# The low part of every second weight load: from a VectorE subtraction to an accumulating DMA

## The chip, the cores and the metric

The kernel runs on one core of one Trainium2 chip. Its time is the device time of one execution in microseconds (us); lower is better. The engines are named as in the profile: PE (TensorE: matmuls; PEld are its weight loads), ACT (ScalarE), DVE (VectorE), POOL (GpSimd), SP (SyncE, which here issues the DMAs).

## The reference: what is computed

Two layers of a decoder over 256 tokens of width 2048, in float32. Layer 0 mixes a causal multi-scale pooling with attention to a memory of 256 tokens; layer 1 has differential attention over shared keys and values, and memory attention again. Each layer ends with a squared-ReLU feed-forward of width 8192. Most of the work is products of the 256 tokens with large weight matrices, used once each:

```python
for i in range(DEPTH):                       # 2
    u = rms_norm(x, mix_norm[i]) @ w_in[i]   # 2048 x 2048
    ...
    x = x + jnp.concatenate([token_out, mem_out], axis=-1) @ w_out[i]
    x = x + squared_relu_mlp(rms_norm(x, ffn_norm[i]), w_ff1[i], w_ff2[i])   # 2048 x 8192 x 2048
```

## The kernel before

**The weights are a stream.** The host lays all weight matrices out as 5796 blocks of 128 x 128 in the order of their use, 8 blocks (1024 columns, 512 KB) to one load: 725 loads, called halves here. The class `Feed` (lines 42 to 100) streams them. `load` issues the DMA of a half from SP into one of 4 buffers named raw (line 60). `fill` works by quarters of 4 blocks (512 columns, two to a half): it makes a high part `hi` by a cast to the matmul's input type float32r on ACT (line 76), and a low part `lo`, what the cast lost, by a subtraction on DVE (line 77); each has 4 buffers of one quarter. `fill(q)` runs before quarter q is used and prepares the quarters up to q + 3 (`AHEAD`); each quarter first asks for the loads up to three halves further on (line 72).

**The matmuls.** The activations are split into a high and a low part as well, side by side (512 columns). `a_part` (lines 216 to 224) and the second matrix of the feed-forward (lines 495 and 496) take two matmuls to a block: `hi` with 512 columns, `lo` with 256. Where the tokens are the output rows, `wide_step` (lines 236 to 244) takes six matmuls of 512 columns to a quarter.

**The order of the work.** Each engine works through its own queue in the order of the program, and the program is written as the stream goes: `fill` is called from the matmul loops, and other work is hung between the quarters by `at` and `tick` (lines 121 to 127). An engine's queue stands still while its first instruction waits for a buffer, a load or another engine. A buffer is given to the next tile of its name in turn, once the last reader of the old tile is done.

**The feed-forward** (`ffn`, lines 460 to 513) is the largest part: in each of the two layers 4 passes of `up` (first matrix, 16 chunks of 16 blocks, that is two halves each) and 4 of `down` (second matrix, the same size). A chunk of `up` ends with a copy on ACT (line 473), an addition and a product on DVE (lines 475 and 476, the latter through the helper of line 141), a square and a cast on ACT (lines 478 and 479) and a subtraction on DVE (line 480). A chunk of `down` ends with two additions on DVE (lines 451 and 452). Squares for the row norms are summed on POOL (`add_square`, lines 437 to 448). In layer 1 the memory is loaded again into raw buffers (`mem_again`, lines 681 to 688).

Of the kernel before, what the change touches and what calls it, by code (L numbers as in the profile page):

```python
# [10 lines left out]
F32 = mybir.dt.float32  # L11
F32R = mybir.dt.float32r
BF16 = mybir.dt.bfloat16
AF = mybir.ActivationFunctionType
ALU = mybir.AluOpType
# [3 lines left out]
P = 128  # L19
T = 256  # L20
# [8 lines left out]

# columns of the parameter array  # L30
G_MIX, G_MEM, G_FFN, G_KV = 0, 32, 64, 96
G_PS, G_MQ, G_MK, G_QN, G_KN, G_SUB = 112, 124, 126, 128, 129, 130
G_QR, G_KR = 131, 163
NPAR = 195
# columns of the constant array
C_ID, C_MASK, C_COS, C_SIN, C_INV = 0, 128, 256, 288, 320
# [4 lines left out]

class Feed:
    """Streams the weights in the order of use: load, split into a high and a low part."""

    AHEAD = 3

    def __init__(self, nc, wst, wpool):
        self.nc, self.wst, self.wpool = nc, wst, wpool
        self.order = []
        self.pos = 0  # L50
        self.loaded = 0
        self.raw = {}
        self.split = {}
        self.done = 0

    def load(self, upto):
        while self.loaded < min(upto, NH):
            h = self.loaded
            n = min(1024, (NBLK - 8 * h) * P)
            t = self.wpool.tile([P, 1024], F32, tag="raw", bufs=4, name=f"raw{h}")  # L60
            step = 512 if h == 0 else 1024
            for c in range(0, n, step):
                m = min(step, n - c)
                self.nc.sync.dma_start(t[:, c : c + m], self.wst[h, :, c : c + m])
            self.raw[h] = t
            self.loaded += 1

    def fill(self, q):
        nq = NBLK // 4
        while self.done < min(q + 1 + self.AHEAD, nq):  # L70
            i = self.done
            self.load(i // 2 + 4)
            src = self.raw[i // 2][:, (i % 2) * 512 : (i % 2) * 512 + 512]
            hi = self.wpool.tile([P, 512], F32R, tag="hi", bufs=4, name=f"hi{i}")
            lo = self.wpool.tile([P, 512], F32R, tag="lo", bufs=4, name=f"lo{i}")
            self.nc.scalar.copy(hi, src)  # L76
            self.nc.vector.tensor_sub(lo, src, hi.bitcast(F32))  # L77
            self.split[i] = (hi, lo)
            if i % 2:
                del self.raw[i // 2]  # L80
            self.done += 1
# [22 lines left out]
def trunk(ctx: ExitStack, tc: tile.TileContext, xT, memT, par, lam, cst, wst, yT):  # L104
# [11 lines left out]

# [1 line left out]
    pend = {}  # L118
# [13 lines left out]

# [1 line left out]
    def vt(name, bufs=8):  # L134
        return tp.tile([P, T], F32, tag="v", bufs=bufs, name=name)
# [6 lines left out]

# [1 line left out]
    param = cp.tile([P, NPAR], F32, name="param")  # L144
# [37 lines left out]
    def rsqrt(out, mean):  # L182
        """out = 1/sqrt(mean + EPS), [128, 256], mean in PSUM; one Newton step."""
        l = vt("rs_l")
        nc.scalar.activation(l, mean, AF.Ln, bias=eps)
        h = vt("rs_h")
        nc.scalar.activation(h, l, AF.Exp, bias=lnc, scale=-0.5)
        t = vt("rs_t")
        nc.scalar.activation(t, h, AF.Square)
        t2 = vt("rs_t2")  # L190
        stt(t2, mean, EPS, t, ALU.add, ALU.mult)
        stt(out, t2, 3.0 * CN * CN, h, ALU.subtract, ALU.mult, reverse0=True)

    def rsqrt_cols(out, v):
        """out = 1/sqrt(v), a few columns of SBUF, v holding EPS already"""
        n = v.shape[-1]
        w = [tp.tile([P, 16], F32, tag="w8", bufs=8, name="rc")[:, :n] for _ in range(4)]
        nc.scalar.activation(w[0], v, AF.Ln)
        nc.scalar.activation(w[1], w[0], AF.Exp, bias=lnc, scale=-0.5)
        nc.vector.tensor_mul(w[2], w[1], w[1])  # L200
        nc.vector.tensor_mul(w[3], w[2], v)
        stt(out, w[3], 3.0 * CN * CN, w[1], ALU.subtract, ALU.mult, reverse0=True)
# [11 lines left out]

# [1 line left out]
    def a_part(ps, w, l, n, ks, xs, first=True, last=True):  # L216
# [9 lines left out]
    def c_tile(ps, w, l, n, ks, xs):  # L226
        """as a_part, with all three products summed in ps[:, :256]"""
        for i, k in enumerate(ks):
            hi, lo = feed.block((w, l, k, n, 1))
            nc.tensor.matmul(ps[:, 0:T], hi, xs[:, k, 0:T], start=i == 0, stop=False)  # L230
            nc.tensor.matmul(ps[:, 0:T], hi, xs[:, k, T : 2 * T], start=False, stop=False)
            nc.tensor.matmul(ps[:, 0:T], lo, xs[:, k, 0:T], start=False, stop=i == len(ks) - 1)
            if feed.pos % 4 == 0:
                tick()
# [14 lines left out]

# [1 line left out]
    def rstd_from(name):  # L251
# [6 lines left out]
    def columns(name):  # L258
        """1/rms of the tokens, token by partition, and its square"""
        st = stat("tc_" + name)  # L260
        for i in range(2):
            nc.tensor.matmul(
                st[:, 2 * i : 2 * i + 2], acc[name][:, i * P : i * P + P], ones_d[:, 0:2],
                start=True, stop=True,
            )
        v = tp.tile([P, 2], F32, tag="m2", bufs=12, name="cv")
        nc.vector.tensor_scalar_add(v, st[:, 0:4].rearrange("p (a b) -> p a b", b=2)[:, :, 0], EPS)
        col = cp.tile([P, 2], F32, tag="c_" + name, name="c_" + name)
        rsqrt_cols(col, v)
        col2 = cp.tile([P, 2], F32, tag="d_" + name, name="d_" + name)  # L270
        nc.vector.tensor_mul(col2, col, col)
        return col, col2

# [1 line left out]
    def key_rows(ps, cols, d):  # L275
        """ps: two token tiles [128, 512] in PSUM; returns them with heads of d normalised"""
        n = 512 // d
# [19 lines left out]
    def query_rows(ps, cols, d):  # L297
        """the two token tiles as they are, and y[token, (t, head)], the scale of their scores"""
        raw = tp.tile([P, 2, 512], F32, tag="rows", bufs=2, name="qrow")
# [53 lines left out]
    def turn_rows(raw, i, dst, g):  # L353
        """chunks i, i+1 of the rows -> dst [128 features, 2, 256 tokens], times g"""
        t4 = pp.tile([P, 2, T], F32, tag="t", bufs=1, name="tr")
        for c in range(2):
            for t in range(2):
                nc.tensor.transpose(
                    t4[:, c, t * P : t * P + P], raw[:, t, (i + c) * P : (i + c) * P + P], ident
                )  # L360
        nc.scalar.activation(dst, t4, AF.Copy, scale=g)

# [1 line left out]
    def mem_query(src, gq, cols):  # L364
        """src PSUM [128 d, 256]: the queries of one head before their norm, which scales
        the scores; returns them times the gain, and that scale"""
        q = tp.tile([P, T], F32, tag="q", bufs=2, name="mq")
# [21 lines left out]
    def mem_head(q, y, k, v, e, pT, out, lag):  # L389
        """q [128 d, 256] and the scale y[token, block] of its scores; k [128 d, 256],  # L390
        v(mb) -> [128 m, 128 d]; out: split chunk"""

# [42 lines left out]

# [1 line left out]
    def add_square(key, src, first, act=False):  # L437
        """adds the square of a chunk to acc[key]"""
        if first:
            acc[key] = tp.tile([P, T], F32, tag="acc", bufs=2, name="acc")  # L440
            nc.gpsimd.tensor_mul(acc[key], src, src)  # L441
            return
        sq = tp.tile([P, T], F32, tag="psq", bufs=2, name="psq")
        if act:
# [13 lines left out]

# [1 line left out]
    def ffn(l, xs, sz):  # L460
# [53 lines left out]

    # =============== layer 0 ===============
    big = sp.tile([P, 6144], F32, tag="big", name="big0")
# [24 lines left out]

    # keys and values of the memory together, one block row after another
    mem_chunk(0)
# [92 lines left out]
    def out_tiles(l, cat, lead, ks, fx, between):  # L636
        """the output projection; three chunks start on the parts in `lead`, ks come last"""
        first = [mmt("wo") for _ in range(3)]
# [34 lines left out]

    # =============== layer 1 ===============
    kv = sp.tile([P, 6144], F32, tag="big", name="big1")
# [5 lines left out]
    def mem_again(p):  # L681
        t = wp.tile([P, 4, T], F32, tag="raw", bufs=4, name="memraw1")
        nc.sync.dma_start(t, memT[:, 4 * p : 4 * p + 4, :])
        for k in range(4):
            at(
                6 + 2 * k,
                lambda k=k: split_gain(mems1[:, 4 * p + k, :], t[:, k, :], gcol(G_MEM + 16 + 4 * p + k)),
            )
# [63 lines left out]

    # -lambda and the gain behind the heads
    lp = lamt.rearrange("p (a d) -> p a d", a=4)
# [206 lines left out]
```

## Time and profile before

| | us |
|---|---|
| time, median of 2 runs (2113.99 to 2115.19) | 2114.59 |
| span of the profiled execution, first to last instruction | 2112.8 |
| PE busy | 2099.1 (99%) |
| PEld busy | 1814.1 (86%) |
| DVE busy | 1485.7 (70%) |
| ACT busy | 1196.4 (57%) |
| POOL busy | 126.5 (6%) |
| DMA engines, mean busy share of the weights' queue | 56.6% |

No time of its own was kept for the profiled execution beside its span; the median of the runs stands 1.8 us above that span. In rows of groups, "out<-in" names the tiles, x the number of instructions, then come busy us, mean ns of one, and the idle time before them with what ended it. In rows of stretches each engine's busy us stands with its number of instructions, then the granted PE clock, the busy share of the DMA engines and GB/s. In a timeline a row has its start, its duration, engine, line and operation.

### The profile page before, as it was taken

The page shows a single profiled execution, that of the slowest core. Times are in us where ns is not written, and L with a number is a line of the kernel's source. Part 1 is how long each engine was busy: PE and PEld are TensorE (multiplying, and loading weights), DVE is VectorE, ACT ScalarE, POOL GpSimd, SP SyncE. Part 2 cuts the span into 40 slices and gives each one's busy share as a digit, 9 for nine tenths or more (in the row PEclk, how much of TensorE's full clock was granted, in tenths as well). Part 3 has the DMA queues.
Part 4 walks back from the last instruction along what each step waited for, and adds up shares of the span by engine and source line. Part 5 has one row for each costly group of instructions (what it writes and reads, how often), then busy time and mean ns, then how long its engine had stood idle before and what let it go on. Part 6 is the DMA issues. An engine that isn't in the chain of part 4 may idle for free.

```text
span 2112.8 us, 33195 instructions
## 1 busy us (share of the span) xinstructions
PE 2099.1 (99%) x11758; PEld 1814.1 (86%) x11758; DVE 1485.7 (70%) x2788; ACT 1196.4 (57%) x2351; POOL 126.5 (6%) x145
## 2 busy tenths in 40 slices
PE   8999999999999999999999999999999999999999
PEld 6788888888888888888888778888888888888888
DVE  8787876766666666687755687876676666666665
ACT  6665566654564564455655577556664565465443
POOL 7001300000000000032000000310000000000000
PEclk9999999999999999999999999999999999999999
DMA  7546555555555555556565432555555555555564
GB/s 246 181 155 188 187 189 190 190 190 189 192 190 190 191 190 191 189 184 197 188 227 191 142 116 95 179 185 190 190 190 191 191 190 190 189 190 190 189 205 160
DMA packets 110471, 390.81 MB, mean 185 GB/s; under 512 B 12256, under 2 KB 14944, under 8 KB 110304
## 3 DMA queue, kind: packets, MB, share of 16 engines
q1 hardware_dynamic: 110304, 388.69, 56.6%
q8 instruction: 92, 1.51, 0.3%
q14 instruction: 75, 0.61, 0.1%
HBM read 386.54 MB, written 2.10 MB: 184 GB/s over the span
## 4 chain that ended last, share of the span: by engine, by line
PE 97%; DVE 1%; DMA 1%; ACT 1%; issue 0%; SPq 0%; DVEq 0%; ACTq 0%
PE ff L219 22%; PE ff L495 22%; PE ff L220 11%; PE ff L496 11%; PE wo L219 6%; PE wo L220 3%; PE u L219 2%; PE u L220 1%; PE k L241 1%; PE q L241 1%; PE k L243 1%; PE v L241 1%; PE k L242 1%; PE v L242 1%; PE v L243 1%; PE q L243 1%
## 5 line engine op out<-in xcount | busy, mean ns | idle before, releaser
L77 DVE TENSOR_TENSOR lo<-raw,hi 128x512 fp32r<-128x512 f32 x1449 | 1018.8, 707 | 495.4 <-ACT hi L76 469.9
L76 ACT CAST hi<-raw 128x512 fp32r<-128x512 f32 x1449 | 898.3, 621 | 808.3 <-PE ff L495 355.7
L219 PE MATMUL ff<-fx,hi 128*128 128x512 f32 x2048 | 710.9, 393 | 0.0
L495 PE MATMUL ff<-z,hi 128*128 128x512 f32 x2032 | 704.7, 392 | 0.0
L220 PE MATMUL ff<-fx,lo 128*128 128x256 f32 x2048 | 570.4, 279 | 0.0
L496 PE MATMUL ff<-z,lo 128*128 128x256 f32 x2032 | 565.9, 279 | 0.0
L219 PEld LDWEIGHTS ff<-fx,hi 128*128 128x128 f32 x2048 | 383.5, 187 | 86.8
L495 PEld LDWEIGHTS ff<-z,hi 128*128 128x128 f32 x2032 | 380.5, 187 | 86.0
L220 PEld LDWEIGHTS ff<-fx,lo 128*128 128x128 f32 x2048 | 385.7, 188 | 0.1
L496 PEld LDWEIGHTS ff<-z,lo 128*128 128x128 f32 x2032 | 382.7, 188 | 0.0
L219 PE MATMUL wo<-cat,hi 128*128 128x512 f32 x512 | 182.3, 400 | 0.0
L220 PE MATMUL wo<-cat,lo 128*128 128x256 f32 x512 | 143.8, 281 | 0.0
L219 PEld LDWEIGHTS wo<-cat,hi 128*128 128x128 f32 x512 | 96.1, 188 | 23.9 <-DVE cat L141 0.3
L220 PEld LDWEIGHTS wo<-cat,lo 128*128 128x128 f32 x512 | 96.8, 189 | 0.1
L480 DVE TENSOR_TENSOR z<-ff_z,z 128x256 fp32r<-128x256 f32 x128 | 54.5, 426 | 40.8 <-ACT z L479 40.7
L219 PE MATMUL u<-xs,hi 128*128 128x512 f32 x192 | 69.7, 405 | 0.0
L441 POOL TENSOR_TENSOR acc<-resid 128x256 f32<-128x256 f32 x4 | 3.6, 894 | 1096.1 <-DVE resid L452 625.5
L451 DVE TENSOR_TENSOR resid<-resid,ff 128x256 f32<-128x256 f32 x127 | 53.5, 421 | 21.9 <-PE ff L496 20.4
L448 POOL TENSOR_TENSOR acc<-acc,psq 128x256 f32<-128x256 f32 x75 | 65.1, 873 | 20.0 <-ACT psq L445 15.2
L478 ACT ACTIVATE ff_z<-ff_y 128x256 f32<-128x256 f32 x128 | 53.5, 418 | 21.7 <-DVE ff_y L141 21.7
L141 DVE SCALAR_TENSOR_TENSOR ff_y<-ff_y,r_x 128x256 f32<-128x256 f32 x128 | 54.6, 426 | 4.3
L452 DVE TENSOR_TENSOR resid<-resid,ff 128x256 f32<-128x256 f32 x127 | 53.5, 421 | 4.3
(243 smaller groups left out, 1954.2 us busy)
## 6 DMA issues: line engine op xcount, KB each, us to landing
raw<-in_w SPq DMA_DIRECT2D x723, 512.0 KB, 3.4
resid<-in_x SPq DMA_DIRECT2D x8, 256.0 KB, 4.5
memraw<-in_mem SPq DMA_DIRECT2D x4, 512.0 KB, 4.7
out_y<-resid SPq DMA_DIRECT2D x16, 128.0 KB, 2.9
memraw<-in_mem SPq DMA_DIRECT2D x7, 256.0 KB, 4.5
raw<-in_w SPq DMA_DIRECT2D x3, 256.0 KB, 3.4
memraw<-in_mem SPq DMA_DIRECT2D x2, 128.0 KB, 3.1
const<-in_cst SPq DMA_DIRECT2D x1, 168.0 KB, 4.0
```

The lines of the kernel that those rows point to most:

```text
L76: self.nc.scalar.copy(hi, src)
L77: self.nc.vector.tensor_sub(lo, src, hi.bitcast(F32))
L141: nc.vector.scalar_tensor_tensor(out=out, in0=a, scalar=s, in1=b, op0=op0, op1=op1, **kw)
L219: nc.tensor.matmul(ps, hi, xs[:, k, :], start=first and i == 0, stop=False)
L220: nc.tensor.matmul(ps[:, T : 2 * T], lo, xs[:, k, 0:T], start=False, stop=last and i == len(ks) - 1)
L241: nc.tensor.matmul(ps[t], xl, hi, start=k == 0, stop=False)
L243: nc.tensor.matmul(ps[t], xh, lo, start=False, stop=k == NK - 1)
L448: nc.gpsimd.tensor_add(acc[key], acc[key], sq)
L451: nc.vector.tensor_add(resid[:, n, :], resid[:, n, :], ps[:, 0:T])
L480: nc.vector.tensor_sub(z[:, i, T : 2 * T], z2, z[:, i, 0:T].bitcast(F32))
L495: nc.tensor.matmul(ps, hi, z[:, i, :], start=a, stop=False)
L496: nc.tensor.matmul(ps[:, T : 2 * T], lo, z[:, i, 0:T], start=False, stop=b)
```

## The change

Odd halves from 9 to 721 (`summed`) get their low part another way. ACT casts the whole half to `his` in one copy of 1024 columns, ACT multiplies `his` by -1 into `los`, and a DMA issued from POOL loads the same half from memory a second time and adds it to `los` on its way. Even halves, and the first 8 and the last, are split as before. The copy, the product and the DMA of a half are issued 6 quarters ahead (`EARLY`) by `begin`. To make room in on-chip memory, several pools of buffers are smaller: raw 3 in place of 4, hi and lo 2 each in place of 4, beside 2 buffers each of his and los of one half; the small tiles of `vt` 5 in place of 8, psq 1 in place of 2. Comments are taken out, which moves line numbers. The diff, cut to what acts:

```diff
     AHEAD = 3
+    EARLY = 6
...
+        self.begun = 0
+        self.high = {}
+
+    def summed(self, h):
+        return h % 2 == 1 and 8 <= h < NH - 2
 
     def load(self, upto):
...
-            t = self.wpool.tile([P, 1024], F32, tag="raw", bufs=4, name=f"raw{h}")
+            t = self.wpool.tile([P, 1024], F32, tag="raw", bufs=3, name=f"raw{h}")
...
+    def begin(self, upto):
+        while self.begun < min(upto, NH):
+            h = self.begun
+            if self.summed(h):
+                self.load(h + 1)
+                hi = self.wpool.tile([P, 1024], F32R, tag="his", bufs=2, name=f"his{h}")
+                self.nc.scalar.copy(hi, self.raw[h])
+                lo = self.wpool.tile([P, 1024], F32R, tag="los", bufs=2, name=f"los{h}")
+                self.nc.scalar.mul(lo, hi.bitcast(F32), -1.0)
+                self.nc.gpsimd.dma_start(lo, self.wst[h], accum_op=ALU.add)
+                self.high[h] = hi, lo
+            self.begun += 1
+
     def fill(self, q):
         nq = NBLK // 4
         while self.done < min(q + 1 + self.AHEAD, nq):
             i = self.done
-            self.load(i // 2 + 4)
-            src = self.raw[i // 2][:, (i % 2) * 512 : (i % 2) * 512 + 512]
-            hi = self.wpool.tile([P, 512], F32R, tag="hi", bufs=4, name=f"hi{i}")
-            lo = self.wpool.tile([P, 512], F32R, tag="lo", bufs=4, name=f"lo{i}")
-            self.nc.scalar.copy(hi, src)
-            self.nc.vector.tensor_sub(lo, src, hi.bitcast(F32))
+            self.load(i // 2 + 3)
+            self.begin((i + self.EARLY) // 2)
+            h, c = i // 2, slice((i % 2) * 512, (i % 2) * 512 + 512)
+            src = self.raw[h][:, c]
+            if self.summed(h):
+                hi, lo = (x[:, c] for x in self.high[h])
+            else:
+                hi = self.wpool.tile([P, 512], F32R, tag="hi", bufs=2, name=f"hi{i}")
+                self.nc.scalar.copy(hi, src)
+                lo = self.wpool.tile([P, 512], F32R, tag="lo", bufs=2, name=f"lo{i}")
+                self.nc.vector.tensor_sub(lo, src, hi.bitcast(F32))
             self.split[i] = (hi, lo)
...
-    def vt(name, bufs=8):
+    def vt(name, bufs=5):
...
-        sq = tp.tile([P, T], F32, tag="psq", bufs=2, name="psq")
+        sq = tp.tile([P, T], F32, tag="psq", bufs=1, name="psq")
...
-        t = wp.tile([P, 4, T], F32, tag="raw", bufs=4, name="memraw1")
+        t = wp.tile([P, 4, T], F32, tag="raw", bufs=3, name="memraw1")
```

More of the change, by code (lines that the diff above doesn't have):

```diff
@@ L71, in fill @@
             i = self.done
-            self.load(i // 2 + 4)
-            src = self.raw[i // 2][:, (i % 2) * 512 : (i % 2) * 512 + 512]
-            hi = self.wpool.tile([P, 512], F32R, tag="hi", bufs=4, name=f"hi{i}")
-            lo = self.wpool.tile([P, 512], F32R, tag="lo", bufs=4, name=f"lo{i}")
-            self.nc.scalar.copy(hi, src)
-            self.nc.vector.tensor_sub(lo, src, hi.bitcast(F32))
+            self.load(i // 2 + 3)
[9 more added lines that the diff above has]
+                self.nc.vector.tensor_sub(lo, src, hi.bitcast(F32))
             self.split[i] = (hi, lo)
             if i % 2:
-                del self.raw[i // 2]
+                del self.raw[h]
+                self.high.pop(h, None)
             self.done += 1
```

## The prediction

> **What bounds the kernel now.** I read the page first (busy times, chain, groups), then the stretch of one feed-forward stage, then the tile of the loaded weights.
>
> ```profile
> span 2112.8 us, 33195 instructions
> ...
> PE 2099.1 (99%) x11758; PEld 1814.1 (86%) x11758; DVE 1485.7 (70%) x2788; ACT 1196.4 (57%) x2351; POOL 126.5 (6%) x145
> ...
> PE 97%; DVE 1%; DMA 1%; ACT 1%; issue 0%; SPq 0%; DVEq 0%; ACTq 0%
> ...
> L77 DVE TENSOR_TENSOR lo<-raw,hi 128x512 fp32r<-128x512 f32 x1449 | 1018.8, 707 | 495.4 <-ACT hi L76 469.9
> L76 ACT CAST hi<-raw 128x512 fp32r<-128x512 f32 x1449 | 898.3, 621 | 808.3 <-PE ff L495 355.7
> ```
>
> TensorE (PE) is busy in 2099.1 of 2112.8 us and carries 97% of the chain. The splitting of the weights on ACT and DVE waits for PE and not the reverse. So the kernel can gain at most the 13.7 us in which PE is idle, 0.6%, unless its matmuls change, and the diff touches none. Relief for DVE (70% busy) is worth nothing here. What counts is whether weights still come in time. The next row, busy times by stretch, gives the pace at which PE eats them.
>
> ```profile
> core 0: us, PE busy (x) PEld busy (x) DVE busy (x) ACT busy (x) POOL busy (x), PEclk, DMA share, GB/s
> 400.00:800.00 400.00, 400.00 (x2310) 352.69 (x2309) 267.75 (x473) 219.60 (x409) 0.00 (x0) 1.00 0.58 190
> ```
>
> Two matmuls go to a block: 1155 blocks in 400 us, 0.346 us each. A load ("half", 8 blocks) lasts 2.77 us on PE, two halves 5.54 us.
>
> **The change, part by part.** From half 9 to half 721 every odd half, 357 of them, becomes "summed" (S); even ones stay "plain" (P). I write P1 S1 P2 S2 for their order of use. S loses two casts and two subtractions and gains a copy and a multiplication by -1 of 1024 columns on ACT, and one DMA issued by POOL that adds the load to the result. By these rows from the groups with shapes kept apart,
>
> ```profile
> L475 DVE TENSOR_TENSOR ff_y<-ff,ff_c 128x256 f32<-128x256 f32 x128 | 53.5, 418 | 0.0
> ...
> L141 DVE SCALAR_TENSOR_TENSOR ff_y<-ff_y,r_x 128x256 f32<-128x256 f32 x128 | 54.6, 426 | 4.3
> ...
> L478 ACT ACTIVATE ff_z<-ff_y 128x256 f32<-128x256 f32 x128 | 53.5, 418 | 21.7 <-DVE ff_y L141 21.7
> ...
> L479 ACT CAST z<-ff_z 128x256 fp32r<-128x256 f32 x128 | 52.0, 406 | 4.1
> L473 ACT COPY ff_c<-ff 128x256 f32<-128x256 f32 x128 | 46.6, 364 | 0.0
> ...
> L283 ACT ACTIVATE ksq<-krow 128x512 f32<-128x512 f32 x10 | 6.3, 631 | 0.0
> ```
>
> a cast grows by (621-406)/256 = 0.84 ns a column, so the copy of 1024 takes 621+512x0.84 = 1051 ns; an activation by 0.83, so the multiplication takes 631+512x0.83 = 1056 ns. ACT goes up by 357x(1.05+1.06-2x0.62) = 310 us to 1507, DVE down by 357x2x0.707 = 505 to 981. No engine but PE fills the span, and busy time decides nothing.
>
> The buffers decide. Raw buffers go from 4 to 3, so the load of S2 takes the place of P1 and must wait for the last reader of P1, the subtraction of its second quarter on DVE. And ACT works in program order: copy of S2, multiplication of S2, cast, cast of P2, copy of S3. The casts of P2 thus stand behind the copy of S2, which waits for the load of S2, which waits for P1. That closes a ring which gives one turn for each pair of halves, without PE in it. Its steps come from these rows: the tile of the raw weights in a quiet stretch, then a timeline.
>
> ```profile
> L77 DVE TENSOR_TENSOR lo<-raw,hi x73: 683/692/693, 599.4 to 699.1; 128x512 fp32r<-128x512 f32 x73
> L76 ACT CAST hi<-raw x73: 615/622/627, 600.0 to 699.9; 128x512 fp32r<-128x512 f32 x73
> ...
> DMA to landing us min/median/max: 3.1/3.3/4.1
> ```
>
> ```profile
> 799.70 0.62 ACT L76 CAST hi<-raw 128x512 fp32r<-128x512 f32 x1 [0.61 <-PE ff L219]
> ...
> 800.36 0.69 DVE L77 TENSOR_TENSOR lo<-raw,hi 128x512 fp32r<-128x512 f32 x1 [0.54 <-ACT hi L76]
> ...
> 801.08 8.65 SPq L64 DMA_DIRECT2D raw<-in_w  x4
> ```
>
> Hops: ACT to DVE 800.36-800.32 = 0.04, DVE to SP 801.08-801.05 = 0.03; for ACT to ACT I take 0.03 and for landing to ACT 0.04, after these. One turn where PE runs the second matrix of the feed-forward: end of P1's subtraction, hop 0.03, load 3.3, hop 0.04, copy 1.05, hop 0.03, multiplication 1.06, two casts 1.24, hop 0.04, subtraction 0.69: **7.48 us against PE's 5.54**. In the first matrix the copy L473 stands between multiplication and casts, and L475, L141 stand on DVE before the two subtractions. The way over DVE is the longer: the last part is 0.36+0.04+0.42+0.03+0.43+0.69+0.69 = 2.66 in place of 1.97, and the turn 8.17. For the other stages, whose ACT and DVE have as much side work, I take 8.17 too.
>
> What the accumulating DMA adds to this ring is its traffic. It starts after the multiplication, 2.0 us before the next S load is issued. No row shows such a DMA. The nearest are two plain loads in close order, in the DMA queue's timeline and the landings of the same two windows, and the highest rate:
>
> ```profile
> 1075.84 0.33 SPq L64 DMA_DIRECT2D raw<-in_w  x1
> ```
>
> ```profile
> raw<-in_w SPq DMA_DIRECT2D x1, 512.0 KB, 3.4
> ```
>
> ```profile
> 1076.63 0.33 SPq L64 DMA_DIRECT2D raw<-in_w  x1
> ```
>
> ```profile
> raw<-in_w SPq DMA_DIRECT2D x1, 512.0 KB, 4.0
> ```
>
> The first landed at 1079.24 as if alone, the second at 1080.63: a load occupies the DMA engines for about 1.3 us (1.39 here, 1.25 at the 419 GB/s of the busiest slice below), and 2.0 us of its 3.3 are latency.
>
> ```profile
> GB/s 0 151 231 348 232 348 392 408 419 399 224 385 339 284 14 44 350 347 373 354 219 367 67 216 221 63 318 143 11 281 57 90 356 333 283 79 384 111 314 224
> ```
>
> An accumulate reads the weights and the old value, so I take twice, 2.6 us. If POOL and the queue need 1 to 2 us before data flows, those 2.6 us meet the 1.3 us of the next S load. Bounds on the delay: 0 if they pass each other; 2.6 if the load must wait for all of it. I take 1.3, an even share of the engines while both run: nearest to the second load above, which waited for the part of its neighbour that was still running. Nothing excludes a slower accumulate; that is a rival.
> One rule speaks against the change. The Trainium skill, "Collectives: The Full Stack", section on the bandwidth ceiling, says that a summing DMA costs no extra arithmetic but reads two sources on the same read ring, so it ran at about half the rate of a copy. By it an accumulate would take twice a plain load; no run here shows it yet. The Trainium skill, "DMA: Bandwidth & Descriptors", section on issuing engines, adds that POOL's DMAs run on the same 16 engines as SP's; by it the collision is real, and the delay of 0 would need luck in timing.
>
> Latency of the accumulate itself (L, from the end of the multiplication) is not in the ring: PE gets S late but evenly. It enters only through the two buffers of the copied S: S3's copy waits until PE is done with S1, two turns for 2.14+L+2.77, so L counts only above 13.5 us at a turn of 9.2.
>
> Smaller parts, together: casts of P wait for PE four quarters back as before (2 buffers over half the quarters). The 8 to 5 and 2 to 1 buffers serve work that has a whole turn of slack; should squares on POOL come late behind the waiting DMA issue, the row statistic at the end of a stage waits one turn, four times, under 40 us. On SP the load of P3 stands behind the waiting load of S2, lands about 4.0+1.3 us after its issue, and is wanted 6 us after it.
>
> **Sum.** At its start the kernel is not yet in pairs:
>
> ```profile
> 0.00:29.00 29.00, 16.69 (x51) 10.20 (x52) 14.01 (x16) 9.52 (x16) 0.94 0.80 279
> ```
>
> 51 matmuls with high parts by 29 us, 4 a quarter: half 8 starts near 33 us; with 10 us at the end the 357 pairs take 2070 us, 5.80 each. The feed-forward has 128 pairs with each matrix (8 passes of 16 chunks of 2 halves), 101 pairs remain. Mean turn with 1.3 us of delay: (128x8.78 + 229x9.47)/357 = 9.22. Increase 357x(9.22-5.80) = 1221 us. On the profiled 2112.8 that is 3334; the median of the runs stands 1.8 above that span, so **3336 us**. Delay 0 gives 2872, delay 2.6 gives 3800. With the fastest landing (3.1) and no side work in the ring it would be 7.28 a turn, 2643.
>
> **Rivals.** (1) The other side: PE stays the bound and the time stays at 2115. The ring would have to close in 5.54 us, so the load would have to land 1.36 us after its issue; the fastest in the quiet stretch took 3.1. Chance 0.04, with 0.01 of it for a gain over 2%, which the 0.6% of idle PE hardly allows.
> (2) The clock. PE would be idle over 3 us a turn, and this happened early in the run:
>
> ```profile
> 21.52 0.64 PE L243 MATMUL mk<-lo,mems 128*128 128x512 f32 x1 [1.87 <-DVE lo L77]
> ...
> 22.00:24.00 2.00, 2.00 (x6) 1.62 (x5) 2.00 (x3) 0.62 (x1) 1.84 (x3) 0.50 0.20 33
> ```
>
> After a gap of 1.87 us the granted clock was 0.50. If it stayed there, a pair would take 2x5.80 = 11.6 us and the kernel 2114.6+357x5.80 = 4185. Half a clock for only 3 us a turn costs PE 1.5 us and hides in its idle time. The Trainium skill, "TensorE: Matmul & The Clock Gate", section on the HAM clock gate, wants an idle window of about 3.4 us first; the trace did it after less. Chance 0.08.
> (3) The accumulate is itself the bound: slow in POOL's issue or in the DMA engines. It decides above L = 13.5 us; at L = 20 a turn is 12.5 us and the time 2114.6+357x6.7 = 4500. No row speaks for it or against it. Chance 0.10.
> (4) That the DMAs are not issued at all is excluded: POOL's queue holds 357 of them.
>
> **How the numbers follow.** The ring with its collision has 0.78, own range 2643 to 3800, likeliest 3336. The range for 8 in 10 runs from 2750 to 4000: it leaves out rival 1 (0.04), the thin low end of the ring (0.04) and most of rivals 2 and 3 (0.12). A difference under 2% can't be told from none in this measurement: slower 0.96, within 2% 0.03, faster 0.01.
>
> **What would show it.** Right: SP's load issue waits for DVE's subtraction once a pair; ACT's longest wait is the copy of S for the raw load; PE busy near 65%, waiting for the S low part; S loads land in about 4.6 us, not 3.3. Wrong: PE still at 99%; ACT waiting for PE rather than the load; PEclk near 5 in most slices; or S loads landing in 3.3 with PE waiting on accumulates that land after 14 us.

## The result and the profile after

The changed kernel takes 2430.01 us (median of 2 runs, 2424.87 to 2435.16) against 2114.59 before: a ratio of 1.1488, 95% interval 1.1429 to 1.1548. Slower was forecast; 3336 us was not. The profiled execution spans 2433.1 us, and its rows are read against that span.

The page of the changed kernel: engines, the load of the DMA engines in 40 slices, the DMA queues, the chain of work that ended last, by engine and by line.

```profile
span 2433.1 us, 32615 instructions
...
PE 2207.2 (91%) x11758; PEld 1847.2 (76%) x11758; DVE 1014.9 (42%) x2074; ACT 1440.5 (59%) x2351; POOL 422.8 (17%) x502
...
DMA  8889999999998999999879965999999998898997
...
q0 software_dynamic: 51408, 187.19, 45.2%
q1 hardware_dynamic: 110304, 388.69, 44.7%
...
DMA 45%; PE 33%; ACT 10%; issue 9%; POOL 2%; DVE 1%; ACTq 0%; POOLq 0%; DVEq 0%
DMA los<-in_w 37%; DMA raw<-in_w 8%; ACT his L82 6%; PE ff L522 6%; PE ff L246 5%; PE ff L523 3%; PE ff L247 3%; ACT los L84 3%; PE wo L246 2%; PE u L246 1%; PE wo L247 1%; PE q L270 1%; PE q L268 1%; PE q L269 1%; PE v L270 1%
```

PE has become an engine that waits a little: it was idle for 13.7 us and is now for 225.9 (2433.1 - 2207.2); its busy time grew by 108 us with the same 11758 matmuls. The chain was 97% PE and is 45% DMA, 37% of it accumulates on their way and 8% plain loads. The two queues are the reason to look at: q1 (all loads, from SP) holds 44.7% of the span of the 16 DMA engines, 1.50 us for each of 725 loads (some 40 smaller transfers of the same queue are counted in); q0 (the accumulates, from POOL) 45.2%, that is 0.452 x 2433.1 / 357 = **3.08 us each**. Together they fill 89.9%, and 0.93 in the stretch of the feed-forward below.

Groups and DMA issues of the changed kernel, then a stretch of the feed-forward (columns as in the prediction).

```profile
L82 ACT CAST his<-raw 128x1024 fp32r<-128x1024 f32 x357 | 375.1, 1051 | 840.9 <-PE ff L522 289.5
...
L85 POOL DMA_DIRECT2D los<-in_w x357 | 309.0, 865 | 1952.6 <-ACT los L84 961.5
...
L84 ACT ACTIVATE los<-his 128x1024 fp32r<-128x1024 f32 x357 | 378.2, 1060 | 9.7
...
raw<-in_w SPq DMA_DIRECT2D x723, 512.0 KB, 5.3
los<-in_w POOLq DMA_DIRECT2D x357, 512.0 KB, 7.2
```

```profile
400.00:800.00 400.00, 364.49 (x1983) 308.68 (x1981) 143.51 (x283) 230.44 (x348) 53.78 (x63) 0.98 0.93 245
```

From issue to landing, a plain load now takes 5.3 us (3.4 before), an accumulate 7.2. In 400 us PE does 1983 matmuls where it did 2310, with the DMA engines at 0.93 where they were at 0.58. What PE waits for is shown by its three longest waits (us in total, times, longest):

```profile
PE ff L523 <- DMA los<-in_w: 86.2, 68, 3.5
PE ff L247 <- DMA los<-in_w: 56.9, 69, 4.8
PE v L270 <- DMA los<-in_w: 23.2, 7, 6.3
```

All rows of this kind together make 214 of PE's 226 idle us: nearly every wait of PE ends with the landing of an accumulate.

The prediction's ring asks which buffer a load waits for. These are timelines of the copy of one summed half, of the load issued behind it with its landing, of the copy of the next summed half, and of the next plain half; the second copy `his` ends at 700.26, the subtraction `lo` at 703.73.

```profile
692.96 1.05 ACT L82 CAST his<-raw 128x1024 fp32r<-128x1024 f32 x1 [1.65 <-DMA raw<-in_w]
```

```profile
694.04 0.33 SPq L72 DMA_DIRECT2D raw<-in_w  x1
```

```profile
raw<-in_w SPq DMA_DIRECT2D x1, 512.0 KB, 5.1
```

```profile
699.21 1.05 ACT L82 CAST his<-raw 128x1024 fp32r<-128x1024 f32 x1 [2.04 <-DMA raw<-in_w]
700.29 0.33 SPq L72 DMA_DIRECT2D raw<-in_w  x1
```

```profile
702.45 1.28 DVE L103 TENSOR_TENSOR lo<-raw,hi 128x512 fp32r<-128x512 f32 x2
...
703.76 0.33 SPq L72 DMA_DIRECT2D raw<-in_w  x1
```

One load goes out 0.03 us after the copy of a summed half, the next 0.03 us after the last subtraction of a plain one, and so on in turn. Which load is which is told by its landing: the one issued at 694.04, when the copy of one summed half had ended at 694.01, landed 5.1 us later, and the copy of the next summed half, which had waited for a load, began at 699.21. So the summed halves hand a raw buffer from one to the next, and it is let go by the copy on ACT; the plain halves share the other two. The ring of the prediction, in which the load of S2 waits for P1, is not in this kernel.

### The profile page after: what moved, and what is told of

Same layout as the page of the kernel before. It is cut to its first block, busy times and chain, and to the rows that moved or that the text cites. A ratio compares the mean times of both kernels' runs of the same rounds, so it can differ in the third digit from the quotient of the medians.

```text
span 2433.1 us, 32615 instructions
## 1 busy us (share of the span) xinstructions
PE 2207.2 (91%) x11758; PEld 1847.2 (76%) x11758; DVE 1014.9 (42%) x2074; ACT 1440.5 (59%) x2351; POOL 422.8 (17%) x502
## 3 DMA queue, kind: packets, MB, share of 16 engines
q0 software_dynamic: 51408, 187.19, 45.2%
q1 hardware_dynamic: 110304, 388.69, 44.7%
## 4 chain that ended last, share of the span: by engine, by line
DMA 45%; PE 33%; ACT 10%; issue 9%; POOL 2%; DVE 1%; ACTq 0%; POOLq 0%; DVEq 0%
DMA los<-in_w 37%; DMA raw<-in_w 8%; ACT his L82 6%; PE ff L522 6%; PE ff L246 5%; PE ff L523 3%; PE ff L247 3%; ACT los L84 3%; PE wo L246 2%; PE u L246 1%; PE wo L247 1%; PE q L270 1%; PE q L268 1%; PE q L269 1%; PE v L270 1%
## 5 line engine op out<-in xcount | busy, mean ns | idle before, releaser
L82 ACT CAST his<-raw 128x1024 fp32r<-128x1024 f32 x357 | 375.1, 1051 | 840.9 <-PE ff L522 289.5
L85 POOL DMA_DIRECT2D los<-in_w x357 | 309.0, 865 | 1952.6 <-ACT los L84 961.5
L103 DVE TENSOR_TENSOR lo<-raw,hi 128x512 fp32r<-128x512 f32 x735 | 525.5, 735 | 254.7 <-ACT hi L101 233.4
L101 ACT CAST hi<-raw 128x512 fp32r<-128x512 f32 x735 | 434.8, 615 | 63.0 <-PE v L269 19.9
L84 ACT ACTIVATE los<-his 128x1024 fp32r<-128x1024 f32 x357 | 378.2, 1060 | 9.7
L522 PE MATMUL ff<-z,his 128*128 128x512 f32 x1016 | 382.6, 410 | 0.0
L523 PE MATMUL ff<-z,los 128*128 128x256 f32 x1016 | 302.4, 298 | 86.6 <-DMA los<-in_w 86.2
L246 PE MATMUL ff<-fx,his 128*128 128x512 f32 x1024 | 369.6, 396 | 0.0
L246 PE MATMUL ff<-fx,hi 128*128 128x512 f32 x1024 | 365.3, 396 | 0.0
L522 PE MATMUL ff<-z,hi 128*128 128x512 f32 x1016 | 362.8, 396 | 0.0
L246 PEld LDWEIGHTS ff<-fx,hi 128*128 128x128 f32 x1024 | 192.0, 188 | 45.2
L522 PEld LDWEIGHTS ff<-z,hi 128*128 128x128 f32 x1016 | 191.5, 188 | 45.2
```

Of the source, the lines that this page charges most:

```text
L82: self.nc.scalar.copy(hi, self.raw[h])
L84: self.nc.scalar.mul(lo, hi.bitcast(F32), -1.0)
L85: self.nc.gpsimd.dma_start(lo, self.wst[h], accum_op=ALU.add)
L246: nc.tensor.matmul(ps, hi, xs[:, k, :], start=first and i == 0, stop=False)
L522: nc.tensor.matmul(ps, hi, z[:, i, :], start=a, stop=False)
L523: nc.tensor.matmul(ps[:, T : 2 * T], lo, z[:, i, 0:T], start=False, stop=b)
```

## The experiments

Theories: **A**, the 16 DMA engines are full, about 6.1 us of their time per pair of halves (2 x 1.50 + 3.08) against 5.54 on PE; **B**, a ring through the 2 buffers of his and los (copy, product, accumulate, PE's use, and the buffer is free for the next copy but one); **C**, a ring through the one raw buffer of the summed halves (copy, load, next copy). Each time is a median, each ratio is to the kernel before on the same chip.

**e1, the traffic alone.** The kernel before (all halves plain, VectorE subtracts), with raw, `vt` and psq as small as in the changed kernel (hi and lo keep 4 buffers), and an accumulate per odd half that nobody reads:

```diff
+                flag = self.wpool.tile([P, 1], F32, tag="flag", bufs=4, name=f"flag{h}")
+                self.nc.scalar.copy(flag, hi[:, 0:1].bitcast(F32))
+                self.nc.gpsimd.tensor_copy(pad[:, 0:1], flag)
+                self.nc.gpsimd.dma_start(pad, self.wst[h], accum_op=ALU.add)
```

> The kernel before, with the small pools and the 3 raw buffers of the changed one, and beside its own work one accumulating DMA of 512 KB for every second load into two spare buffers that nobody reads. PE never waits for it. Theory A, the DMA engines are full (6.0 us of their time for a pair of loads against 5.54 us on PE): 2300 to 2450 us, loads landing in over 5 us and PE waiting for them. Theory B, the ring through the two buffers of the summed halves (copy, product, accumulate of 7.2 us, PE), and theory C, the ring through the one raw buffer that the summed halves hand on: neither ring is here, so 2115 to 2170 us, though loads land later.

2377.48 us, 1.1223 (1.1149 to 1.1298). Theory A alone foresaw it. Its page and the stretch:

```profile
q1 hardware_dynamic: 110304, 388.69, 49.3%
q0 software_dynamic: 51408, 187.19, 42.1%
...
DMA 50%; PE 24%; DVE 11%; ACT 10%; issue 4%; POOL 1%; ACTq 0%; SPq 0%; DVEq 0%; POOLq 0%
...
raw<-in_w SPq DMA_DIRECT2D x723, 512.0 KB, 6.2
```

```profile
400.00:800.00 400.00, 376.61 (x2017) 310.24 (x2016) 229.05 (x411) 188.21 (x411) 81.07 (x126) 0.99 0.95 248
```

No matmul reads these accumulates, and yet the plain loads land in 6.2 us and half the chain is waiting for DMA. The changed kernel's row above has nearly the same matmuls, DMA share and GB/s.

**e2, his and los by quarters** (4 buffers each, 256 KB DMAs), so that a copy waits for PE's use of one quarter:

```diff
-                hi = self.wpool.tile([P, 1024], F32R, tag="his", bufs=2, name=f"his{h}")
+                for c in (slice(0, 512), slice(512, 1024)):
+                    hi = self.wpool.tile([P, 512], F32R, tag="his", bufs=4, name=f"his{h}")
```

> The changed kernel with the summed halves made by quarters: two copies, two products and two accumulating DMAs of 256 KB, into 4 buffers of one quarter each. Same memory, same bytes by DMA; a buffer comes free after half the PE time and the way round is shorter. Theory B: most of the loss goes, 2115 to 2250 us. Theory A: the bytes are the same, 2350 to 2450 us. Theory C: the raw buffer is still handed on after the copies, 2380 to 2450 us.

2446.71, 1.1541 (1.1494 to 1.1587): no gain, as A and C foresaw, DMA share 1.00 to 1.02 in the feed-forward. B alone is not the limit. It is not excluded as a part: the second reads in two pieces took more of the DMA engines (3.14 us for each summed half, and loads 1.63), which may have used up what the shorter ring gave.

**e3, a fourth raw buffer** and loads one half earlier (room from smaller pools of other tiles):

```diff
-            t = self.wpool.tile([P, 1024], F32, tag="raw", bufs=3, name=f"raw{h}")
+            t = self.wpool.tile([P, 1024], F32, tag="raw", bufs=4, name=f"raw{h}")
-            self.load(i // 2 + 3)
+            self.load(i // 2 + 4)
```

> The changed kernel with 4 raw buffers in place of 3 and loads asked for one half earlier; the room comes from four small pools used in attention and norms. Theory C: loads no longer wait for the copy of the summed half just before, ACT's waits for the load (230 us) go, 2115 to 2280 us. Theories A and B: within 2% of the changed kernel, 2380 to 2470 us.

2370.21, 1.1153 (1.1084 to 1.1221): 60 us less than the changed kernel, 10 us under the range of A and B and far above that of C. ACT's copies wait 17.0 us for raw loads where they waited 229.8, so C's ring is gone and was worth about 60 of the 315 us.

**e4, the changed kernel without its DMA:** a subtraction on DVE in place of product and accumulate.

```diff
-                self.nc.scalar.mul(lo, hi.bitcast(F32), -1.0)
-                self.nc.gpsimd.dma_start(lo, self.wst[h], accum_op=ALU.add)
+                self.nc.vector.tensor_sub(lo, self.raw[h], hi.bitcast(F32))
```

> The changed kernel with the low part of the summed halves made by one DVE subtraction of 1024 columns in place of product and DMA; all buffers and the early issue stay. All three theories need the second read: 2115 to 2150 us. If the smaller pools, the longer copy or ACT's order of work cost by themselves, over 2180 us.

2163.36, 1.0194 (1.0153 to 1.0236), DMA share 0.54, 13 us above the range given: buffers and whole-half copies cost about 41 us by the ratio (48 between medians of different chips); the rest comes with the second read.

**e5 to e8, what of the traffic it is.** All are e1 with another DMA; e7 and e8 need one more buffer and take it from other small pools. e5 has none, e6 a plain one, e7 the same plain one for every half (two per pair), e8 an accumulate from on-chip memory:

```diff
-                self.nc.gpsimd.dma_start(pad, self.wst[h], accum_op=ALU.add)
+                self.nc.gpsimd.dma_start(pad, self.wst[h])
...
+                self.nc.gpsimd.dma_start(pad, self.pad[2], accum_op=ALU.add)
```

> The kernel before with the smaller pools (3 raw buffers, loads one half earlier trimmed to 3, small tiles 5 and 1) and the one-column flags on ACT and POOL of e1, but with no extra DMA. It is the base line of e1, e6 and e7. Theory A (DMA engines full): 2 x 1.47 = 2.9 us of engine time per pair against 5.5 on PE, so 2115 to 2165 us. Had the smaller pools and the flags made e1's 262 us, this would be 2300 to 2400.

> As e1, but the unused extra DMA of every odd half (512 KB) is a plain load and not an accumulating one; same issue, same pacing, same bytes from memory. Theory A: 3 x 1.47 = 4.4 us of DMA engine time per pair, below PE's 5.54, so 2115 to 2180 us, raw loads landing in about 4 us. Rival D (not engine time but the third DMA per pair from a second queue, or its 512 KB from memory, costs the time): as e1, 2300 to 2450.

> As e6, but one unused plain extra load for every half and not only every odd one, so two per pair (three extra buffers in rotation, 4 small tiles). Theory A: 4 x 1.47 = 5.9 us of engine time per pair, nearly the 6.0 of e1; at e1's share of busy engines (0.915) a pair takes 6.4 us and the kernel 43 + 357 x 6.4 = 2330 us, expected 2270 to 2400. Rival E (an accumulate slows the stream by something of its own, such as holding the queue between its read and its write, and not by engine time): 2115 to 2200.

> As e1, but the unused accumulating DMA takes its 512 KB from a third buffer in on-chip memory and not from the weights in HBM. Theory A with the accumulate's time in the engines (reading two sources and writing one): as e1, 2320 to 2450 us, about 3 us of engine time per accumulate. Rival F (the second read from HBM is what is scarce): 2115 to 2180.

e5 2127.88, 1.0038 (1.0010 to 1.0067); e6 2149.30, 1.0172 (1.0124 to 1.0219); e7 2275.81, 1.0783 (1.0713 to 1.0854), without its profiled execution, which took 2306.48; e8 2289.35, 1.0826 (1.0777 to 1.0875), 31 us under A's range and far above F's. The stretch of the feed-forward in e6, with one plain load more per pair:

```profile
400.00:800.00 400.00, 398.81 (x2268) 346.64 (x2267) 263.84 (x469) 221.67 (x475) 67.76 (x142) 1.00 0.81 281
```

In e7, with two plain loads more:

```profile
400.00:800.00 400.00, 386.80 (x2121) 323.86 (x2121) 243.85 (x431) 207.41 (x499) 122.55 (x265) 1.00 0.94 349
```

In e8, with one accumulate more from on-chip memory:

```profile
400.00:800.00 400.00, 389.75 (x2139) 326.33 (x2137) 242.15 (x434) 199.07 (x437) 86.07 (x134) 1.00 0.98 263
```

One plain load more costs little (share 0.81). Two cost 7.8% (0.94), nearly as much as an accumulate that reads nothing from HBM (0.98, 8.3%). So most of the cost is the engines' time, in which an accumulate counts for 1.65 to 2.05 loads. HBM's bytes do not order the times: e7 moved 349 GB/s and ran faster than e1 with 248. Between e8 and e1 88 us are left, with only 38 us more engine time; they may be the read from HBM, which was not taken apart. The Trainium skill, "Collectives: The Full Stack", on the bandwidth ceiling, has the summing step of a reduce-scatter read two sources on one ring, at about half the rate of a copy. For the accumulates here the ratio is near that: 3.08 against 1.50 us in the changed kernel, 2.81 against 1.62 in e1, 2.69 against 1.63 in e8.

**e11, a plain second read in the changed kernel** in place of the accumulate; the sum is left out, and the low part is the weights themselves.

```diff
-                self.nc.gpsimd.dma_start(lo, self.wst[h], accum_op=ALU.add)
+                self.nc.gpsimd.dma_start(lo, self.wst[h].bitcast(F32R))
```

> The changed kernel with a plain second load in place of the accumulating one, in the same place behind the product: the low part of every summed half is overwritten by the weights themselves, so the output is not the reference's. Theory A: 2 x 1.53 + 1.58 = 4.6 us of engine time per pair as in e6; e6's 1.7% and up to 2% for the pools (e4) give 2140 to 2200 us. If what costs time is that PE has to wait for a load that starts late, behind copy and product, and not the engines' time, it stays at 2350 to 2450.

2184.08, 1.0339 (1.0310 to 1.0368), los landing in 4.9 us. Its stretch of the feed-forward:

```profile
400.00:800.00 400.00, 398.65 (x2265) 346.64 (x2264) 163.27 (x322) 261.68 (x397) 36.95 (x70) 1.00 0.87 279
```

As A has it: same place, same bytes, 1.74 us of engine time per second read instead of 3.08 (0.285 x 2180.0 / 357), and nearly four fifths of the loss are gone. The run does not tell A from B, since with the engine time the landing fell as well, from 7.2 to 4.9 us.

**e9, the prediction's order of buffers made real:** three raw buffers handed out strictly in turn.

```diff
-            t = self.wpool.tile([P, 1024], F32, tag="raw", bufs=3, name=f"raw{h}")
+            t = self.wpool.tile([P, 1024], F32, tag=f"raw{self.turn % 3}", bufs=1, name=f"raw{h}")
+            self.turn += 1
```

> The changed kernel with its three raw buffers handed out strictly in turn (load h takes the buffer of load h-3), so that the load of every summed half must wait for the DVE subtraction of a plain one, as the prediction had it. Theory H (the ring was costed rightly and failed only because the changed kernel hands a buffer on from summed half to summed half): a turn of 7.48 us (8.17 with side work) with loads landing in 3.3, up to 2 us more with loads landing in 5.3 as in the changed kernel, so 43 + 357 x 7.92 to 43 + 357 x 9.92 = 2870 to 3590 us, and SP waits for DVE before every load of a summed half. Rival G (the ring was costed wrongly as well, and full DMA engines set the time whoever gets which buffer): 2400 to 2480.

3121.0, 1.4755 (1.4713 to 1.4796): the order in which buffers are handed on is worth 691 us. The waits of SP, then the chain:

```profile
SPq L74 <- DVE lo L105: 1021.6, 336, 13.3
```

```profile
DMA 41%; PE 37%; issue 16%; ACT 4%; DVE 1%; POOL 1%; SPq 0%; POOLq 0%; ACTq 0%; DVEq 0%
DMA los<-in_w 37%; PE ff L524 8%; PE ff L248 8%; PE ff L525 5%; PE ff L249 5%; DMA raw<-in_w 4%; PE wo L248 2%; ACT los L86 1%; ACT his L84 1%; PE wo L249 1%; PE u L248 1%; ACT hi L103 1%; DVE lo L105 1%; PE u L249 1%; PE s L815 0%
```

The wait for `lo` is there as foretold, but the chain runs over the accumulates (37%) and PE, and only 4% over the raw loads. With the loads late, the copy of a summed half falls behind a cast that waits for PE, and the landing of the accumulate, which the prediction left out of the ring, is inside. So the number came out in its range by luck, through a ring that is only half the predicted one.

**e10, every fourth half,** which by A should have freed the engines.

```diff
-        return h % 2 == 1 and 8 <= h < NH - 2
+        return h % 4 == 1 and 8 <= h < NH - 2
```

> The changed kernel with only every fourth half summed (178 of them) in place of every second. Theory A: per four halves 4 loads of 1.5 and one accumulate of 3.1 us, 9.1 us of engine time against 11.1 on PE, a share of 0.82 as in e6, whose time was 1.7% above before; with up to 2% for the smaller pools (e4) 2130 to 2200 us. A theory in which each accumulate costs the same wherever it stands, (2430-2115)/357 = 0.88 us, gives 2115 + 178 x 0.88 = 2272.

3065.72, 1.4523 (1.4486 to 1.4559): both theories missed by far. The timeline of one turn, 16.82 us for four halves:

```profile
1000.59 0.39 PE L523 MATMUL ff<-z,los 128*128 128x256 f32 x1 [4.00 <-DMA los<-in_w]
...
1006.28 0.63 ACT L101 CAST hi<-raw 128x512 fp32r<-128x512 f32 x1 [9.38 <-PE ff L522]
...
1006.81 1.05 ACT L82 CAST his<-raw 128x1024 fp32r<-128x1024 f32 x1
...
1008.27 1.06 ACT L84 ACTIVATE los<-his 128x1024 fp32r<-128x1024 f32 x1
...
1009.63 0.86 POOL L85 DMA_DIRECT2D los<-in_w  x1 [16.37 <-PE ff L523]
...
1013.39 0.40 PE L522 MATMUL ff<-z,his 128*128 128x512 f32 x1
...
1017.41 0.39 PE L523 MATMUL ff<-z,los 128*128 128x256 f32 x1 [3.62 <-DMA los<-in_w]
```

ACT's cast of a plain quarter waits for one of 2 buffers of hi, that is for PE; the copy of the next summed half stands behind that cast; only then can the accumulate go out (1009.63), 7.7 us ahead of its landing. PE wants it at 1013.39, and every turn it waits 3.6 us. With every second half summed, the same 2 buffers last twice as long in halves; by the order of the program ACT then runs 8 quarters ahead instead of 5. The lead, not full engines, is what fails here (DMA share 0.57). Why an accumulate still takes 7.7 us to land, with 5.2 at best, was not tried.

**e12, e10 with four raw buffers** and loads one half earlier (the edit of e3).

> e10 with four raw buffers and loads one half earlier, as e3 (room from smaller pools of other tiles). Theory A: the share of the engines is 0.82 as in e10; if e4's 2% came from the missing raw buffer it goes, and 2120 to 2160 us are left, the least that a second read of any of the weights can cost here, since PE was busy in 2099 us of 2113 before. If the 2% came from the summed halves' own structure (whole-half copies ahead of the casts), half of it stays: 2140 to 2180.

2320.52, 1.0974 (1.0940 to 1.1007): 745 us back, and still 160 above what A allows. PE's waits for los are mostly gone (16.9 us at the second matrix, 227.0 in e10); ACT's copies wait 305.5 us for raw loads, and the casts stand behind them. That need not be the 160 us, for in e4 such waits make 384.5 us at a time of 2163; the cause stays open.

**e13, e10 with 3 buffers each of hi and lo; e14, the same for the changed kernel.**

```diff
-                hi = self.wpool.tile([P, 512], F32R, tag="hi", bufs=2, name=f"hi{i}")
+                hi = self.wpool.tile([P, 512], F32R, tag="hi", bufs=3, name=f"hi{i}")
```

> e10 with 3 buffers each of hi and lo in place of 2 (room from smaller pools of other tiles, 3 raw buffers as before). In e10 the copy of a summed half stands on ACT behind a cast that waits until PE has done the 6th quarter ahead of that half, so 5 quarters, 6.9 us, are left for cast, copy, cast, product, issue and landing (0.62 + 1.05 + 0.61 + 1.06 + 0.3 + 7.7 = 11.3 us); with 3 buffers it waits for the 9th quarter ahead and 8 are left, 11.1 us. Theory J (the lead, PE waits for the accumulate): nearly all of e10's loss goes, 2130 to 2300 us, PE's waits for los fall from 450 us and more to under 100. If three plain halves in a row are slow for another reason (raw buffers, SP's waits for DVE), it stays above 2800.

> The changed kernel with 3 buffers each of hi and lo in place of 2, and the same smaller pools as e13. Here the copy of a summed half stands behind a cast that waits for the 9th quarter ahead with 2 buffers and with 3 (the order on ACT moves along). Theory A (engines full at 6.1 us per pair): 2370 to 2450 us, as the changed kernel. If the casts' buffers hold up part of the changed kernel: below 2330.

e13 2639.98, 1.2449 (1.2354 to 1.2544); e14 2479.18, 1.1688 (1.1599 to 1.1777). The two rows of waits of e10, then those of e13:

```profile
PE ff L523 <- DMA los<-in_w: 227.0, 64, 4.5
PE ff L247 <- DMA los<-in_w: 210.4, 64, 4.3
```

```profile
ACT his L82 <- DMA raw<-in_w: 592.4, 158, 6.0
...
PE ff L523 <- DMA los<-in_w: 139.5, 64, 3.4
...
PE ff L247 <- DMA los<-in_w: 125.9, 64, 4.7
```

More lead takes 426 us off, so the lead is part of the cause; the forecast of 2130 to 2300 failed, because the copies now wait for the raw loads (592.4 us, 158 times) and the accumulate is late again. e14 gained nothing (29 us above the range given): the changed kernel was not held by these buffers. Why it lost 49 us stays open; the smaller pools that made room for it are also in e3, e7, e8, e12 and e13.

**All runs in one table.** Engine time is the share of both queues times the span, as for q0 and q1 above; PE needs 2099 us.

| kernel | DMA engine time, us | time, us |
|---|---|---|
| before | 1196 | 2114.59 |
| e4, e5 (no second read) | 1144, 1138 | 2163, 2128 |
| e6, e11 (plain, one per pair) | 1670, 1785 | 2149, 2184 |
| e7 (plain, two per pair), e8 (accumulate from on-chip) | 2077, 2142 | 2276, 2289 |
| e3, e1, changed kernel, e14, e2 | 2164, 2180, 2187, 2148, 2303 | 2370, 2377, 2430, 2479, 2447 |
| e12, e13, e10 (every fourth) | 1749, 1680, 1720 | 2321, 2640, 3066 |
| e9 (in turn) | 2238 | 3121 |

Down to the fifth row the time follows the larger of the two resources: below 1800 us of engine time PE sets it within 3.4%, above 2070 it goes up to 8 to 17% over before. Engine time alone does not give the size: e8 and e14 have nearly the same (2142 and 2148) and lie 190 us apart, and the changed kernel takes 11% more than its 2187. In the last two rows waits decide (in e12 what is left stays open): e10 is the slowest but one of all with the engines little more than half busy.

## Why the prediction was right in sign and wrong in size

1. **PE bounds, DVE's relief is worth nothing: right.** DVE fell to 1014.9 us (981 forecast), and nothing came of it. ACT's copy and product took 1051 and 1060 ns (1051 and 1056 forecast), though ACT's busy time came to 1440.5 us and not 1507.

2. **"The load of S2 takes the place of P1 and must wait for the last reader of P1": wrong, the step that failed.** The timeline shows the load of a summed half going out behind ACT's copy of the summed half before (694.04 after 694.01), and a turn of 6.7 us in place of 9.2. The belief that buffers go round in turn, stated in the description of the kernel before as well, does not hold here; the traces show which buffer a load waited for, not the rule by which it was chosen. e9 shows what that belief costs: 3121 us with it, 2430 without. So the kernel did get slower, as forecast, but not through this ring.

3. **The traffic, "I take 1.3, an even share of the engines while both run": the term mis-sized, and put in the wrong place.** The factor of two was right (3.08 to 1.50). But a load was costed at 1.3 us of engine time, from the busiest slice of the run; the queue's own row before, 56.6% of the span (in the table of the profile before), gives 0.566 x 2112.8 / 725 = 1.65. With 1.3 a pair needs 2.6 + 2.6 = 5.2 us, below PE's 5.54, and the engines never look full; with 1.65 it needs 6.6. No rival said "the DMA engines are the next bound"; rival 3 came nearest, but asked for a landing above 13.5 us, and 7.2 was measured. From that row alone, 1196 us of loads plus 357 x 3.3 us of accumulates are 2374 us of engine time, 2.3% below the time measured. That nearness is luck: a load took 1.50 and not 1.65, the engine time was 2187, and the time stands 11% above it.

4. **"Latency of the accumulate itself ... is not in the ring" and "counts only above 13.5 us": wrong.** That limit was worked out for a turn of 9.2 us. At PE's own turn the same sum, two turns for 2.14 + L + 2.77, gives 2 x 5.54 - 4.91 = 6.2 us, and issue and landing took 0.3 + 7.2 = 7.5 in the median. So the two buffers of his and los (theory B) allow no turn under (4.91 + 7.5)/2 = 6.2 us, about the 6.1 that the DMA engines need. With the best landing, 5.2 us, it would be 5.2, and PE's 5.54 would hide it. This sum suggests that the full engines stretch the landing and that the ring of theory B passes this on to PE, whose waits end with accumulates. It is an argument and not shown: no run has more buffers of his and los at the same traffic. e1 shows that the traffic makes most of the loss even where PE waits for no accumulate. In e9, e10 and e13 the landing of the accumulate decides as well.

5. **Landing 4.6, PE 65% busy, a turn of 9.2 us:** measured 5.3, 91%, and (2433.1 - 43) / 357 = 6.7. The clock (rival 2) stayed at a mean of 0.982, which is worth 0.018 x 2433 = 44 us, less than half of the 108 that PE's busy time grew by; the rest is not explained.

e1's traffic (2377.48 - 2127.88 = 250 us over e5) and e4's structure (41 us) make 291 of the 315 us, if the two add, which no run shows. Of e4's 41 us the smaller pools alone (without hi and lo) explain about 8 (e5). What the rest of the 41 is stays open.

## What to carry to other kernels

Before moving an engine's work onto DMA, take the queue's share of the DMA engines from the page and add the new bytes to it, an accumulate at twice a load: when the sum comes near the span, the engines become a bound, whatever engine was relieved. Here kernels with 2077 to 2303 us of engine time took 2276 to 2479. Then ask how long before its use each such DMA can be issued, by following what stands ahead of its inputs in the queue of the engine that makes them. And read from the trace which buffer a load really waits for; half as many accumulates with too short a lead (e10) lost three times as much, 951 us against 315.

## What the runs showed of the hardware

An accumulate of 512 KB took 865 ns of POOL to issue (533 to 537 for a plain load from POOL, e6, e7 and e11), landed in the changed kernel in 5.2 us at best and 7.2 in the median, and held the DMA engines, over all runs, for 2.7 to 3.2 us where a plain load held them for 1.4 to 1.7. A source in on-chip memory hardly changed that (862 ns, 2.69 us). PE's clock fell after a short wait: in the changed kernel, a wait of 2.47 us was followed by a granted clock of 0.50 from 718 to 720 us, and by matmuls at half pace.

```profile
717.17 0.58 PE L523 MATMUL ff<-z,los 128*128 128x256 f32 x1 [2.47 <-DMA los<-in_w]
...
717.98 0.41 PE L523 MATMUL ff<-z,los 128*128 128x256 f32 x1
...
721.26 0.28 PE L523 MATMUL ff<-z,los 128*128 128x256 f32 x1
```

The matmul of 256 columns takes 0.41 us for some 3 us and then 0.28 again. The Trainium skill, "TensorE: Matmul & The Clock Gate", on the HAM clock gate, gives one idle window of about 3.4 us as the condition; here, as at 21.52 us of the kernel before, less was enough.
